# Attention on one Trainium2 core: each query tile's scores in one run of 1280 PSUM columns, with one maximum, one exponential and one sum

## The chip, the core and the metric

The kernel runs as one program on one core of a Trainium2 chip. Five engines work side by side, each through its own instructions strictly in order: PE (TensorE, matmuls and transposes), DVE (VectorE), ACT (ScalarE), POOL (GpSimd) and SP (it issues DMAs). They meet through semaphores. PE writes its results into PSUM, 16 KB for each of 128 partitions, in eight banks of 512 fp32 columns; DVE and ACT read them there. The metric is the device time of one execution in microseconds (us), lower is better.

## The reference, cut to what matters

One layer of a diffusion backbone: a SwiGLU half step, a mixer with 12 heads of latent attention beside a state-space branch, a second SwiGLU half step. All of it is fp32. The change touches only this part, for 1024 query rows (1024 latent tokens) and 1280 keys (256 context tokens and the 1024 latent ones):

```python
def attend(q_nope, q_rope, k_nope, k_rope, v):
    s = (jnp.einsum('bqhd,bkhd->bhqk', q_nope, k_nope)
         + jnp.einsum('bqhr,bkr->bhqk', q_rope, k_rope)).astype(jnp.float32) * ATTN_SCALE
    p = jax.nn.softmax(s, axis=-1).astype(v.dtype)
    return jnp.einsum('bhqk,bkhd->bqhd', p, v)
```

## The kernel before, in words

To keep fp32 accuracy, an operand is split in a high part H and a low part L, and a product is three matmuls (`mm3`: HH, HL, LH, lines 574 to 576). The attention stage runs over 96 query tiles n = 0 to 95 (12 heads with 8 tiles of 128 rows each). For a tile, PE makes 128 x 1280 scores in three chunks: a (512 columns), b (512) and c (256). DVE takes the row maximum, ACT the exponential with that maximum as bias, and the row sum beside it (an ACTIVATE and then an ACTIVATION_READ_ACCUMULATOR); POOL inverts the sum and scales the row. That is the softmax of a tile.

Six tiles later PE begins to turn the probabilities of four tiles (a group) around, one block of 128 keys at a time. I call this step t: four transposes into one of two banks named pt (line 1335), then ACT copies the bank to ptH (line 1338), then DVE subtracts to get ptL (line 59, a helper), which frees the bank. Step v is the two matmuls with the values, o<-ptH and o<-ptL (lines 1349 and 1350). A group has ten steps t and ten steps v, and they alternate. The o bank is copied out by ACT at the end of a group (lines 1357 and 1358).

Nothing is scheduled by a tool here. The order in which each engine gets its instructions is written out in the strings of PLAN, one string for each tile, four strings in a cycle (line 37): a, b and c are chunks of scores of tile n, s is the next step t or v, m and M are the maxima over 1024 and over 256 columns, 1 and 0 are the exponentials over 256 and over 1024 columns of tile n-1, and p is a step of the projections that prepare the next head (queries q, keys k or values v_proj; their results go through the two pt banks too, under the name proj). The tile n=0 uses string 1, n=1 string 2, and so on, so tiles with even n use strings 1 and 3.

PSUM holds the scores in three tiles of the tile framework: scA0 and scA1, 1024 columns each, for even and odd n, and scB, one bank of 512 columns of which even n uses the first 256 and odd n the last 256. The framework adds the semaphore waits: an instruction that writes a tile waits for the readers of what stood there, and so on.

Of the kernel before, what the change touches and what calls it, by code (L numbers as in the profile page):

```python
# [7 lines left out]
F32 = mybir.dt.float32  # L8
F32R = mybir.dt.float32r
I32 = mybir.dt.int32  # L10
AF = mybir.ActivationFunctionType
ALU = mybir.AluOpType
AX = mybir.AxisListType
PSUM = bass.MemoryType.PSUM
DRAM = bass.MemoryType.DRAM
MUL, ADD, SUB, POW = ALU.mult, ALU.add, ALU.subtract, ALU.pow
# [10 lines left out]
NKEY = NT * 128  # L27
# [6 lines left out]
MAGIC = 12582912.0  # L34
GC = 2
LAG = 3
PLAN = "s10bamsspscMs as1ss0bmpcMss s1s0bamspcsMs a10bsmsspcMss".split()
PVLAG = 2
XNP = (1, 3, 5)
XLAG = 2  # L40
# [4 lines left out]
class Kernel:  # L45
# [26 lines left out]
        if name in self.dbg:  # L72
            self.nc.sync.dma_start(self.dbg[name][i], t)

    # ---------------------------------------------------------------- build
    def build(self):
        with self.tc.manual_schedule(), ExitStack() as st:
            self.cst = self.pool(st, "cst")
            self.dram = st.enter_context(self.tc.tile_pool(name="dram", bufs=1, space=DRAM))
            self.small = self.pool(st, "small", bufs=4)  # L80
            ap = self.pool(st, "acc")
            self.flat = ap.tile([128, NT * D], F32, name="acc")
            self.acc = [self.flat[:, t * D:(t + 1) * D] for t in range(NT)]
            self.setup()
            sbig, srow, sattn = ExitStack(), ExitStack(), ExitStack()
            self.big = self.pool(sbig, "big", side="right").tile([128, 80 * 256], F32R, name="big")
            with ExitStack() as sp:
                self.ps = self.pool(sp, "ps", bufs=4, space=PSUM)
                self.ffn1_mix_in(srow)
                self.attn_pools(sattn)  # L90
                self.s5_main(sattn)
            self.attention(sattn)
            srow.close()
            with ExitStack() as sp:
                self.ps = self.pool(sp, "ps2", bufs=4, space=PSUM)
                self.mix_out_ffn2(sbig)
# [37 lines left out]
        self.late = []  # L134
        self.mod = {}

    # ---------------------------------------------------------------- adaln
    def adaln_first(self, pool):
        nc = self.nc
        wm = {}  # L140
# [101 lines left out]
        while self.late:  # L242
            yield 1.0

    # ---------------------------------------------------------------- S5 parameters
    def s5_pre(self, st):
        nc, a = self.nc, self.a
        V, Q = nc.vector, nc.gpsimd
# [275 lines left out]
        self.tt(TB, s, wc, MUL)  # L524
        self.tt(so, TA, TB, ADD)

    # ---------------------------------------------------------------- norm + transpose
    def rstd(self, ss, n, tag):
        w = ss.shape[-1]
        v = self.small.tile([128, w], F32, tag=tag + "v", name="rv")  # L530
        self.ts(v, ss, 1.0 / n, MUL, EPS, ADD)
        r = self.small.tile([128, w], F32, tag=tag + "r", name="rr")
        self.tt(r, v, self.half[:, 0:1].to_broadcast([128, w]), POW, self.nc.gpsimd)
        return r
# [29 lines left out]
            nc.scalar.activation(out=hf[:, :n], in_=t[:, :n], func=AF.Identity, scale=av, bias=bv)  # L564
        self.tt(hL[:, kt, :], hf[:, :n], hH[:, kt, :].bitcast(F32), SUB, nc.gpsimd if kt % 2 else None)

    # ---------------------------------------------------------------- FFN
    def split(self, raw, H, L, eng=None):
        self.nc.scalar.activation(out=H, in_=raw, func=AF.Copy)  # L569
        self.tt(L, raw, H.bitcast(F32), SUB, eng)  # L570
# [331 lines left out]
    def hf(self, pool):  # L902
        return lambda: pool.tile([128, 512], F32, tag="hf", name="hf")

    # ---------------------------------------------------------------- mixer: input projection, latents
    def u_at(self, g):
        return self.acc[(8, 9, 0, 1)[g // 4]][:, 512 + (g % 4) * 128:640 + (g % 4) * 128]

# [114 lines left out]
            for hl in range(2):  # L1023
                self.copy_p(self.kT[1][par][hl][rows], self.kT[0][par][hl][rows].bitcast(F32))

    # ---------------------------------------------------------------- attention: projections
    def attn_pools(self, st):
        nc, a = self.nc, self.a
        wp = self.pool(st, "aw", bufs=2)
# [69 lines left out]
            else:  # L1099
                n -= 1  # L1100

    # ---------------------------------------------------------------- S5
    def s5_main(self, sattn):
        nc, a = self.nc, self.a
        self.proj_bank = lambda: self.bank("gu", "proj")
# [166 lines left out]
            self.prep_steps(1)  # L1272
        self.prep_steps(1000)

    # ---------------------------------------------------------------- attention
    def attention(self, sattn):
        nc, a, acc = self.nc, self.a, self.acc
        Q, V = self.Q, self.V
        self.sq, os, ot = acc[0], acc[8], acc[9]
        P = self.row + [self.flat[:, D + i * NKEY:D + (i + 1) * NKEY] for i in range(4)]  # L1280
        nc.gpsimd.memset(self.sq, 0.0)
        with sattn, ExitStack() as s1:
            psc = self.pool(s1, "psc", space=PSUM)
# [1 line left out]
            ppv = self.pool(s1, "ppv", space=PSUM)  # L1285
            tp = self.pool(s1, "aT", bufs=3)
            P.append(self.pool(s1, "p8").tile([128, NKEY], F32, name="p8"))
            scA = [psc.tile([128, 1024], F32, name=f"scA{i}") for i in range(2)]
            scB = psc.tile([128, 512], F32, name="scB")
            self.proj_bank = lambda: ptp.tile([128, 512], F32, tag="tp", name="proj")  # L1290

            def part(n):
                return scB[:, (n % 2) * 256:(n % 2) * 256 + 256]

            def scores(n, k0, w):
                h, i = divmod(n, 8)
                qs = slice(i * 128, (i + 1) * 128)
                qH, qL = Q[h]
                kH, kL = self.kT[(h // 2) % 2][h % 2]
                o = scA[n % 2][:, k0:k0 + w] if k0 < 1024 else part(n)  # L1300
                ks = slice(k0, k0 + w)
                self.mm3(o, qH[:, qs], qL[:, qs], kH[:, ks], kL[:, ks], True, True)

            Pt, MX = {}, {}

            def rowmax(n, i):
                if i == 0:
                    MX[n] = self.small.tile([128, 2], F32, tag="mx", name="mx")
                nc.vector.tensor_reduce(out=MX[n][:, i:i + 1], in_=part(n) if i else scA[n % 2], axis=AX.X, op=ALU.max,
                                        negate=True)  # L1310
                if i:
                    self.tt(MX[n][:, 0:1], MX[n][:, 0:1], MX[n][:, 1:2], ALU.min)

            SM = {}

            def expo(n, i):
                p, b = P[n % 9], MX[n][:, 0:1]
                if i:
                    SM[n] = self.small.tile([128, 2], F32, tag="sm", name="sm")
                    nc.scalar.activation(out=p[:, 1024:1280], in_=part(n), func=AF.Exp, bias=b, accum_out=SM[n][:, 1:2])  # L1320
                    return
                sm = SM.pop(n)
                nc.scalar.activation(out=p[:, 0:1024], in_=scA[n % 2], func=AF.Exp, bias=b, accum_out=sm[:, 0:1])
                r = self.small.tile([128, 1], F32, tag="mr", name="smr")
                self.tt(sm[:, 0:1], sm[:, 0:1], sm[:, 1:2], ADD, nc.gpsimd)
                self.tt(r, sm[:, 0:1], self.neg1, POW, nc.gpsimd)
                self.ts(p, p, r, MUL, 1.0, MUL, nc.gpsimd)
                Pt[n] = p

# [67 lines left out]
            weights(1)  # L1397
            plan = PLAN
            for n in range(NU + TLAG):
                h, i = divmod(n, 8)  # L1400
                if n < NU and i == 0 and h + 1 < HEADS:
                    for x in prep[h + 1]:
                        next(x)
                    todo = slots(h + 1)
                if n < NU and i == 5:
                    weights(h + 2)
                if n >= TLAG and (n - TLAG) % 4 == 0 and (n - TLAG) // 4 < NU // 4:
                    gr = (n - TLAG) // 4
                    for kt in range(NT):
                        queue.append(("t", gr, kt))  # L1410
                        pend.append(("v", gr, kt))
                        if len(pend) > PVLAG:
                            queue.append(pend.pop(0))
                    if gr == NU // 4 - 1:
                        queue.extend(pend)
                if n < NU:
                    for c in plan[n % len(plan)]:
                        if c == "a":
                            scores(n, 0, 512)
                        elif c == "b":  # L1420
                            scores(n, 512, 512)
                        elif c == "c":
                            scores(n, 1024, 256)
                        elif c == "s":
                            step(1)
                        elif c in "01" and n:
                            expo(n - 1, int(c))
                        elif c == "m":
                            rowmax(n, 0)
                        elif c == "M":  # L1430
                            rowmax(n, 1)
                        elif c == "p" and todo:
                            next(todo.pop(0))
                else:
                    if n == NU:
                        expo(n - 1, 1)
                        expo(n - 1, 0)
                    step(5)
                if n >= 81:
                    next(early, None)  # L1440
# [1 line left out]
                pass  # L1442
            step(1000)

    # ---------------------------------------------------------------- mixer: output, second FFN
    W_AT = ((16, 20), (24, 28), (0, 4), (44, 76), (36, 40), (48, 52), (56, 60), (64, 68))
    O_AT = (32, 34, 8, 14, 10, 12, 72, 74)

# [297 lines left out]
```

## Time and profile before

| What | Before |
|---|---|
| median time of three runs | 2608.74 us (2608.11 to 2609.61) |
| span of the profiled execution | 2608.1 us |
| time of the execution outside the span, by the median | 0.6 us |
| PE busy | 2457.2 us, 94% of the span |
| DVE, POOL, ACT busy | 1711.2, 1091.0, 811.3 us |
| first scores of tile 0 start | 1279.68 us |
| last chunk c of tile 95 ends | 1740.7 us |
| mean granted TensorE clock over the span | 0.981 of full |

The profile shows one execution. Busy times of different engines overlap, so they don't add up to the span; what an engine's wait costs is only seen where the engine that sets the pace sits idle.

### The profile page before, as it was taken

To read this page: it belongs to the slowest core of one execution; us is meant where nothing else is said; L and a number is where in the kernel's file an instruction comes from. 1 tells how busy PE (TensorE), PEld (TensorE's weight loads), DVE (VectorE), ACT (ScalarE), POOL (GpSimd) and SP (SyncE) were. 2 spreads that over 40 slices of the span, in tenths; PEclk is the share of its full clock that TensorE was granted. 3 is DMA by queue.
4 is the path that set the end of the run, shared out by engine and by line. 5 is a ranking of instruction groups with operands and counts; after the bars stand their busy time and mean duration, and the time that the engine had idled before them with its cause. 6 is when DMAs were issued, how large, how long until landed. Compare 5 with 4: busy or idle time off the path is not lost. (4 is left out here: it accounts for less than half of the span.)

```text
span 2608.1 us, 32824 instructions
## 1 busy us (share of the span) xinstructions
PE 2457.2 (94%) x12100; PEld 2009.7 (77%) x12100; DVE 1711.2 (66%) x3096; ACT 811.3 (31%) x1555; POOL 1091.0 (42%) x1010
## 2 busy tenths in 40 slices
PE   7999999998998898898899999989999999999998
PEld 4787888786777677697677777767788888888886
DVE  3588674999999987646688888882444444444433
ACT  4311111111111111343577777772411111111112
POOL 2342222253445345625566676665522222222222
PEclk9999999998999899999999999999999999999999
DMA  7143432112222223414200000014111111111111
GB/s 284 41 153 109 150 110 79 36 46 74 65 74 82 65 66 113 145 26 161 79 6 16 11 16 21 15 61 152 57 57 49 45 45 49 49 49 49 49 41 65
DMA packets 92896, 186.38 MB, mean 71 GB/s; under 512 B 23352, under 2 KB 53304, under 8 KB 91712
## 3 DMA queue, kind: packets, MB, share of 16 engines
q1 hardware_dynamic: 59984, 163.92, 18.3%
q10 hardware_dynamic: 32752, 20.36, 2.5%
q8 instruction: 95, 1.56, 0.2%
q14 instruction: 65, 0.53, 0.1%
HBM read 155.52 MB, written 27.54 MB: 70 GB/s over the span
## 5 line engine op out<-in xcount | busy, mean ns | idle before, releaser
L59 DVE TENSOR_TENSOR acc<-dn,acc 128x512 f32<-128x512 f32 x756 | 509.8, 690 | 282.4 <-PE dn L576 281.9
L59 POOL TENSOR_TENSOR wL<-raw,wH 128x1024 fp32r<-128x1024 f32 x130 | 326.2, 2510 | 762.9 <-ACT wH L569 695.3
L574 PE MATMUL gu<-big,wH 128*128 128x512 f32 (+1 forms) x1056 | 382.8, 363 | 9.0 <-DVE sg L59 6.5
L575 PE MATMUL gu<-big,wH 128*128 128x512 f32 (+1 forms) x1056 | 377.1, 357 | 1.7 <-POOL big L59 1.7
L576 PE MATMUL gu<-big,wL 128*128 128x512 f32 (+1 forms) x1056 | 377.1, 357 | 0.7 <-POOL wL L59 0.7
L574 PE MATMUL dn<-wH,aH 128*128 128x512 f32 x792 | 318.5, 402 | 55.9 <-DVE acc L59 54.9
L575 PE MATMUL dn<-wL,aH 128*128 128x512 f32 x792 | 314.5, 397 | 0.0
L576 PE MATMUL dn<-wH,aL 128*128 128x512 f32 x792 | 314.4, 397 | 0.1
L569 ACT ACTIVATE wH<-raw 128x1024 fp32r<-128x1024 f32 x130 | 137.0, 1054 | 519.5 <-PE dn L576 257.6
L575 PE MATMUL gu<-hL,wH 128*128 128x512 f32 x704 | 276.8, 393 | 3.7 <-POOL hL L59 2.8
L574 PE MATMUL gu<-hH,wH 128*128 128x512 f32 x704 | 277.9, 395 | 0.6 <-ACT hH L559 0.6
L576 PE MATMUL gu<-hH,wL 128*128 128x512 f32 x704 | 276.8, 393 | 0.0
L59 POOL TENSOR_TENSOR aL<-sg,aH 128x512 fp32r<-128x512 f32 (+1 forms) x110 | 137.9, 1263 | 285.5 <-ACT aH L569 285.4
L59 DVE TENSOR_TENSOR sg<-gu,sg 128x512 f32<-128x512 f32 (+1 forms) x110 | 68.1, 634 | 281.4 <-PE gu L576 264.7
L574 PEld LDWEIGHTS gu<-big,wH 128*128 128x128 f32 x1056 | 198.7, 188 | 46.4 <-DVE sg L59 7.0
L575 PEld LDWEIGHTS gu<-big,wH 128*128 128x128 f32 x1056 | 198.7, 188 | 35.8 <-POOL big L59 2.1
L574 PEld LDWEIGHTS dn<-wH,aH 128*128 128x128 f32 x792 | 153.0, 193 | 93.4 <-DVE acc L59 60.7
L576 PEld LDWEIGHTS gu<-big,wL 128*128 128x128 f32 x1056 | 198.5, 188 | 33.5 <-POOL wL L59 1.1
L59 DVE TENSOR_TENSOR ptL<-pt,ptH 128x512 fp32r<-128x512 f32 x240 | 162.9, 686 | 52.9 <-ACT ptH L1338 52.2
L569 ACT ACTIVATE aH<-sg 128x512 fp32r<-128x512 f32 (+1 forms) x110 | 62.9, 587 | 412.9 <-DVE sg L59 399.2
L576 PEld LDWEIGHTS dn<-wH,aL 128*128 128x128 f32 x792 | 152.3, 192 | 34.1 <-POOL aL L59 0.5
L575 PEld LDWEIGHTS dn<-wL,aH 128*128 128x128 f32 x792 | 153.1, 193 | 31.1
(318 smaller groups left out, 4803.1 us busy)
## 6 DMA issues: line engine op xcount, KB each, us to landing
raw<-in_w_gu SPq DMA_DIRECT2D x86, 512.0 KB, 3.2
wmr<-in_w_mod SPq DMA_DIRECT2D x56, 512.0 KB, 4.1
raw<-in_w_down SPq DMA_DIRECT2D x44, 512.0 KB, 3.3
row<-d_s SPq DMA_DIRECT2D x16, 576.0 KB, 3.9
wm<-in_w_mod SPq DMA_DIRECT2D x8, 1024.0 KB, 7.1
d_s<-T ACTq DMA_DIRECT2D x32, 160.0 KB, 2.1
ck<-d_s SPq DMA_DIRECT2D x16, 320.0 KB, 4.9
acc<-in_x SPq DMA_DIRECT2D x8, 512.0 KB, 10.6
```

What stands on the lines that cost most here:

```text
L59: (eng or self.nc.vector).tensor_tensor(out=out, in0=a, in1=b, op=op)
L569: self.nc.scalar.activation(out=H, in_=raw, func=AF.Copy)
L574: mm(out, lhsT=AH, rhs=BH, start=start, stop=False)
L575: mm(out, lhsT=AH, rhs=BL, start=False, stop=False)
L576: mm(out, lhsT=AL, rhs=BH, start=False, stop=stop)
```

## The change

The three PSUM tiles become one, sc, of 2560 columns (five banks). Even tiles use columns 0 to 1279, odd ones 1280 to 2559, so the third bank is shared: its first half belongs to even tiles, its second half to odd ones. The keys of odd tiles are cut at other places so that no chunk crosses a bank: c, the chunk of 256 columns that lies in the shared bank, is still the last one of the tile. One reduction over 1280 columns takes the place of two reductions and a minimum of the two results; one exponential over 1280 columns with its sum takes the place of two; POOL's addition of the two sums is gone. In the strings of PLAN, M is now the only maximum (it stands after c, where the second one stood) and E the only exponential.

```diff
-PLAN = "s10bamsspscMs as1ss0bmpcMss s1s0bamspcsMs a10bsmsspcMss".split()
+PLAN = "sEbasspscMs asEsbspcMss sEsbaspcsMs asEsbsspcMss".split()
+CHUNKS = ({"a": (0, 512), "b": (512, 512), "c": (1024, 256)}, {"a": (256, 512), "b": (768, 512), "c": (0, 256)})
...
-            scA = [psc.tile([128, 1024], F32, name=f"scA{i}") for i in range(2)]
-            scB = psc.tile([128, 512], F32, name="scB")
+            sc = psc.tile([128, 2 * NKEY], F32, name="sc")
...
-            def part(n):
-                return scB[:, (n % 2) * 256:(n % 2) * 256 + 256]
+            def region(n):
+                return sc[:, (n % 2) * NKEY:(n % 2 + 1) * NKEY]
...
-                o = scA[n % 2][:, k0:k0 + w] if k0 < 1024 else part(n)
                 ks = slice(k0, k0 + w)
-                self.mm3(o, qH[:, qs], qL[:, qs], kH[:, ks], kL[:, ks], True, True)
+                self.mm3(region(n)[:, ks], qH[:, qs], qL[:, qs], kH[:, ks], kL[:, ks], True, True)
...
-            def rowmax(n, i):
-                if i == 0:
-                    MX[n] = self.small.tile([128, 2], F32, tag="mx", name="mx")
-                nc.vector.tensor_reduce(out=MX[n][:, i:i + 1], in_=part(n) if i else scA[n % 2], axis=AX.X, op=ALU.max,
-                                        negate=True)
-                if i:
-                    self.tt(MX[n][:, 0:1], MX[n][:, 0:1], MX[n][:, 1:2], ALU.min)
...
+            def rowmax(n):
+                MX[n] = self.small.tile([128, 1], F32, tag="mx", name="mx")
+                nc.vector.tensor_reduce(out=MX[n], in_=region(n), axis=AX.X, op=ALU.max, negate=True)
+
+            def expo(n):
+                p = P[n % 9]
+                sm = self.small.tile([128, 1], F32, tag="sm", name="sm")
+                nc.scalar.activation(out=p, in_=region(n), func=AF.Exp, bias=MX.pop(n), accum_out=sm)
                 r = self.small.tile([128, 1], F32, tag="mr", name="smr")
-                self.tt(sm[:, 0:1], sm[:, 0:1], sm[:, 1:2], ADD, nc.gpsimd)
-                self.tt(r, sm[:, 0:1], self.neg1, POW, nc.gpsimd)
+                self.tt(r, sm, self.neg1, POW, nc.gpsimd)
```

How the instructions and their waits stand in the two built programs is shown at two places. A semaphore is named after the engine that raises it, and the lines of the changed kernel are off by one in the helpers (L574 is L575 there) and by twelve in the steps t and v.

The first place is PE in the kernel before, from the last step t ahead of an odd tile with string 4: the step t, then a and b of the tile (scA_11285 is scA1), then v and t.

```order
L1335 MATMUL pt<-ident,acc 128x128 [waits DVE_49]
L1335 MATMUL pt<-ident,acc 128x128 x3
L574 MATMUL scA_11285<-big,qH 128x512 [waits Activation_49]
L575 MATMUL scA_11285<-big,qH 128x512
L576 MATMUL scA_11285<-big,qL 128x512
L574 MATMUL scA_11285<-big,qH 128x512
L575 MATMUL scA_11285<-big,qH 128x512
L576 MATMUL scA_11285<-big,qL 128x512
L1349 MATMUL o<-ptH,v_11018 128x512 [waits PE_49,Activation_49]
L1350 MATMUL o<-ptL,v_11018 128x512
L1335 MATMUL pt<-ident,acc 128x128 [waits DVE_49]
```

Here a waits for ACT alone; by the value waited for, this is the exponential over 1024 columns of tile n-2, the last reader of scA1. The same place of the changed kernel, on PE:

```order
L1323 MATMUL pt<-ident,acc 128x128 [waits DVE_49]
L1323 MATMUL pt<-ident,acc 128x128 x3
L575 MATMUL sc<-big,qH 128x512 [waits DVE_49]
L576 MATMUL sc<-big,qH 128x512
L577 MATMUL sc<-big,qL 128x512
L1337 MATMUL o<-ptH,v_11018 128x512 [waits PE_49,Activation_49]
L1338 MATMUL o<-ptL,v_11018 128x512
L575 MATMUL sc<-big,qH 128x512 [waits Activation_49]
L576 MATMUL sc<-big,qH 128x512
L577 MATMUL sc<-big,qL 128x512
L1323 MATMUL pt<-ident,acc 128x128 x4
```

The chunk a now waits for DVE, and the step v stands between a and b. By the values waited for, a waits for the maximum of tile n-1 (the reduction over the even half of sc), and b for the exponential of tile n-1. Of the 96 tiles, all 48 odd ones have this wait of a on DVE, and 95 (all but the first) have a wait of their first chunk after E on ACT for the exponential of tile n-1.

The second place is ACT in the kernel before, over the softmaxes of three tiles in a row (acc, p_11283 and then row_9372 are where the probabilities go):

```order
L1320 ACTIVATE acc,sm<-scB,mx 128x256 [waits DVE_49,Pool_49]
L1338 CAST ptH<-pt 128x512 [waits PE_49,Activation_49]
L1323 ACTIVATE acc,sm<-scA_11284,mx 128x1024
L1338 CAST ptH<-pt 128x512 [waits PE_49,Activation_49]
L1338 CAST ptH<-pt 128x512 [waits DVE_49,PE_49]
L1320 ACTIVATE p_11283,sm<-scB,mx 128x256 [waits DVE_49,Pool_49]
L1323 ACTIVATE p_11283,sm<-scA_11285,mx 128x1024
L1338 CAST ptH<-pt 128x512 [waits PE_49,Activation_49]
L1357 COPY acc<-o 64x512 [waits PE_49,Pool_49]
L1358 COPY acc<-o 64x512
```

The exponentials wait for DVE (the maximum) and POOL. The same tiles on ACT in the changed kernel:

```order
L1312 ACTIVATE acc,sm<-sc,mx 128x1280 [waits DVE_49,PE_49,Pool_49]
L1326 CAST ptH<-pt 128x512 [waits PE_49,Activation_49] x2
L1326 CAST ptH<-pt 128x512 [waits DVE_49,PE_49]
L1312 ACTIVATE p_11283,sm<-sc,mx 128x1280 [waits DVE_49,Pool_49]
L1326 CAST ptH<-pt 128x512 [waits PE_49,Activation_49]
L1345 COPY acc<-o 64x512 [waits PE_49,Pool_49]
L1346 COPY acc<-o 64x512
L1326 CAST ptH<-pt 128x512 [waits DVE_49,PE_49]
L1312 ACTIVATE row_9372,sm<-sc,mx 128x1280 [waits DVE_49,PE_49,Pool_49]
```

Every second exponential, that of an even tile n-1, has a wait for PE that was not there: by its value, for the last matmul of chunk a of the odd tile n, which the program issues ahead of it. The copies to ptH that stood between or behind two shorter exponentials now stand behind one longer one.

## Rows read from the trace of the kernel before

**Rows 1.** Busy time by engine from the first scores to the last, with clock:

```profile
core 0: us, PE busy (x) PEld busy (x) DVE busy (x) ACT busy (x) POOL busy (x), PEclk, DMA share, GB/s
1279.68:1740.80 461.12, 433.29 (x2445) 352.08 (x2444) 387.70 (x610) 350.19 (x753) 310.47 (x380) 1.00 0.06 22
```

**Rows 2.** Waits of PE in that stretch: total us, times, longest:

```profile
PE pt L1335 <- DVE ptL L59: 15.2, 31, 1.6
PE scB L574 <- ACT row L1320: 1.1, 3, 0.5
```

**Rows 3.** Groups of DVE and ACT: count, busy us, mean ns:

```profile
L1309 DVE TENSOR_REDUCE mx<-scA 128x1 f32<-128x1024 f32 x96 | 116.7, 1216 | 9.4 <-PE scA L576 8.6
L1309 DVE TENSOR_REDUCE mx<-scB 128x1 f32<-128x256 f32 x96 | 40.1, 417 | 1.2
L59 DVE TENSOR_TENSOR mx<-mx 128x1 f32<-128x1 f32 x96 | 43.2, 450 | 3.3
L59 DVE TENSOR_TENSOR ptL<-pt,ptH 128x512 fp32r<-128x512 f32 x240 | 162.9, 686 | 52.9 <-ACT ptH L1338 52.2
L1338 ACT CAST ptH<-pt 128x512 fp32r<-128x512 f32 x240 | 138.3, 586 | 47.1 <-PE pt L1335 42.6 <-DVE mx L1309 1.1 <-DVE mx L59 1.0
L59 POOL TENSOR_TENSOR sm<-sm 128x1 f32<-128x1 f32 x96 | 18.5, 192 | 108.7 <-ACT row L1323 48.2 <-ACT acc L1323 46.8 <-ACT p L1323 13.0
```

**Rows 4.** Timeline of ACT, softmax of tile 0: start us, duration us:

```profile
1286.79 0.47 ACT L1320 ACTIVATE row<-scB,mx 128x256 f32<-128x256 f32 x1
1287.16 0.19 ACT L1320 ACTIVATION_READ_ACCUMULATOR row<-scB,mx 128x1 f32 x1
1287.26 1.10 ACT L1323 ACTIVATE row<-scA,mx 128x1024 f32<-128x1024 f32 x1
1288.25 0.20 ACT L1323 ACTIVATION_READ_ACCUMULATOR row<-scA,mx 128x1 f32 x1
```

**Rows 5.** Timeline of PE beside it, with idle time and releaser:

```profile
1287.41 0.39 PE L574 MATMUL scB<-big,qH 128*128 128x256 f32 x1 [0.17 <-ACT row L1320]
...
1288.50 0.50 PE L574 MATMUL scA<-big,qH 128*128 128x512 f32 x1 [0.47 <-ACT row L1323]
1288.84 0.40 PE L575 MATMUL scA<-big,qH 128*128 128x512 f32 x1
```

**Rows 6.** Timeline of PE later, steps t and v, then chunk c:

```profile
1523.68 0.27 PE L1335 MATMUL pt<-ident,p 128*128 128x128 f32 x1
1523.79 0.49 PE L1335 MATMUL pt<-ident,row 128*128 128x128 f32 x3
1524.04 0.48 PE L1349 MATMUL o<-ptH,v 128*128 128x512 f32 x1
...
1524.58 0.28 PE L574 MATMUL scB<-big,qH 128*128 128x256 f32 x1
...
1524.82 0.28 PE L576 MATMUL scB<-big,qL 128*128 128x256 f32 x1
1524.93 0.27 PE L1335 MATMUL pt<-ident,p 128*128 128x128 f32 x1
```

**Rows 7.** Timeline of PE, a chunk of 512 columns and the step v behind it:

```profile
1527.50 0.40 PE L574 MATMUL scA<-big,qH 128*128 128x512 f32 x1
...
1527.97 0.40 PE L576 MATMUL scA<-big,qL 128*128 128x512 f32 x1
1528.21 0.40 PE L1349 MATMUL o<-ptH,v 128*128 128x512 f32 x1
```

**Rows 8.** Groups of the projections in that stretch, PE, DVE and ACT:

```profile
L574 PE MATMUL proj<-big,wqH 128*128 128x512 f32 x44 | 18.6, 423 | 1.4 <-ACT wqH L1043 1.2 <-DVE ptL L59 0.2
...
L59 DVE TENSOR_TENSOR big<-proj,big 64x512 fp32r<-64x512 f32 x20 | 13.7, 686 | 6.5 <-ACT big L1073 6.5
...
L1073 ACT CAST big<-proj 64x512 fp32r<-64x512 f32 x20 | 11.6, 580 | 8.4 <-DVE big L59 8.2
```

**Rows 9.** PE alone in two stretches before attention: length, busy, granted clock:

```profile
1190.00:1200.00 10.00, 7.45 (x40) 0.67 0.46 170
...
1240.00:1260.00 20.00, 15.75 (x102) 0.96 0.53 175
```

**Rows 10.** Timeline of PE in an earlier stage, after an idle gap:

```profile
1091.00 0.80 PE L574 MATMUL dn<-wH,aH 128*128 128x512 f32 x1 [2.04 <-DVE acc L59]
1091.59 0.63 PE L575 MATMUL dn<-wL,aH 128*128 128x512 f32 x1
```

More of the change, by code (lines that the diff above doesn't have):

```diff
@@ L36 @@
 LAG = 3
-PLAN = "s10bamsspscMs as1ss0bmpcMss s1s0bamspcsMs a10bsmsspcMss".split()
+PLAN = "sEbasspscMs asEsbspcMss sEsbaspcsMs asEbsspcMss".split()
+CHUNKS = ({"a": (0, 512), "b": (512, 512), "c": (1024, 256)}, {"a": (256, 512), "b": (768, 512), "c": (0, 256)})
 PVLAG = 2
@@ L1299, in scores @@
                 kH, kL = self.kT[(h // 2) % 2][h % 2]
-                o = scA[n % 2][:, k0:k0 + w] if k0 < 1024 else part(n)
                 ks = slice(k0, k0 + w)
-                self.mm3(o, qH[:, qs], qL[:, qs], kH[:, ks], kL[:, ks], True, True)
+                self.mm3(region(n)[:, ks], qH[:, qs], qL[:, qs], kH[:, ks], kL[:, ks], True, True)
             Pt, MX = {}, {}
-            def rowmax(n, i):
-                if i == 0:
-                    MX[n] = self.small.tile([128, 2], F32, tag="mx", name="mx")
-                nc.vector.tensor_reduce(out=MX[n][:, i:i + 1], in_=part(n) if i else scA[n % 2], axis=AX.X, op=ALU.max,
-                                        negate=True)
-                if i:
-                    self.tt(MX[n][:, 0:1], MX[n][:, 0:1], MX[n][:, 1:2], ALU.min)
[L1314 to L1323, printed above, removed]
+            def rowmax(n):
[5 more added lines that the diff above has]
+                nc.scalar.activation(out=p, in_=region(n), func=AF.Exp, bias=MX.pop(n), accum_out=sm)
                 r = self.small.tile([128, 1], F32, tag="mr", name="smr")
-                self.tt(sm[:, 0:1], sm[:, 0:1], sm[:, 1:2], ADD, nc.gpsimd)
-                self.tt(r, sm[:, 0:1], self.neg1, POW, nc.gpsimd)
+                self.tt(r, sm, self.neg1, POW, nc.gpsimd)
                 self.ts(p, p, r, MUL, 1.0, MUL, nc.gpsimd)
@@ L1417, in attention @@
                     for c in plan[n % len(plan)]:
[L1418 to L1423, printed above, removed]
+                        if c in "abc":
+                            scores(n, *CHUNKS[n % 2][c])
                         elif c == "s":
                             step(1)
[L1426 to L1429, printed above, removed]
+                        elif c == "E" and n:
+                            expo(n - 1)
                         elif c == "M":
-                            rowmax(n, 1)
+                            rowmax(n)
                         elif c == "p" and todo:
@@ L1435, in attention @@
                     if n == NU:
-                        expo(n - 1, 1)
-                        expo(n - 1, 0)
+                        expo(n - 1)
                     step(5)
```

## The prediction, made before the changed kernel ran

> **What bounds the kernel now.** The change touches the attention stage alone, so I read that stretch by itself, from the first scores at 1279.68 us to the last chunk of scores at 1740.8. PE is busy for 433.3 of its 461.1 us at the full granted clock [rows 1]; DVE (387.7) and ACT (350.2) have room. So PE sets the pace, and 27.8 us, its idle time, is all that shorter work on other engines can give back there. The waits of PE say where some of that goes: 15.2 us for ptL on DVE before a step t, and about 1 us in the row for the exponentials [rows 2]. PE almost never waits for softmax: the scores of tile n wait for an exponential of n-2 in scA that is long done, and only c shares a PSUM tile with n-1.
>
> **What the change removes.** A tile's maxima now cost DVE 1.216 + 0.417 us and the minimum 0.450 [rows 3]. From the two reductions one column costs (1.216 - 0.417)/768 = 1.04 ns, so 1280 columns cost 1.48 us: 0.60 us less per tile, 58 us over 96 tiles. ACT's two exponentials run from 1286.79 to 1288.45, 1.66 us; alone they take 0.56 and 1.19 to the end of the accumulator's reading [rows 4], so one of 1280 columns takes 1.19 + 0.21 = 1.40: 25 us less in all. POOL saves 0.192 us 96 times, 18 us [rows 3]. All of that is taken from engines that don't set the pace. PE's own matmuls stay the same in number and width.
>
> **What it adds: waits.** The order rows decide this case. In the changed program a of every odd tile waits for the maximum of tile n-1, though it writes other banks; the exponential of n-1 then waits for a; and in every tile the first chunk after E waits for the exponential of n-1. The two halves of sc are one tile for the waits, so the double buffer is gone: scores of n and softmax of n-1 take turns. PE runs in order, so everything behind the waiting chunk, the steps t and v too, is held.
>
> The price of one turn, from rows. A follower starts 0.05 us after its releaser: ACT's reading ends at 1287.35 and 1288.45 [rows 4], PE starts at 1287.41 and 1288.50 [rows 5]. The first matmul after a stall takes 0.34 to the second (1288.50 to 1288.84) [rows 5], others 0.235 (two from 1527.50 to 1527.97), the last one ends 0.40 after its start [rows 7]. From the end of c of n-1 to the first chunk after E:
>
> - even tile n: 0.05 + maximum 1.48 + 0.05 + exponential 1.40 + 0.05 = 3.03 us;
> - odd tile n: 0.05 + 1.48 + 0.05 + a (0.34 + 0.235 + 0.40 = 0.97) + 0.05 + 1.40 + 0.05 = 4.05 us.
>
> PE has little to do meanwhile. A step t takes 0.36 to 0.38 us and a v behind it 0.54 (1523.68, 1524.04, 1524.58) [rows 6], a v behind other matmuls 0.47. Between c and the held chunk stand two to four such steps in an even tile, 1.3 to 1.8 us, and two or three with a in an odd one, some 2.0.
>
> Queues make it longer, so I replay one cycle of four tiles by hand, without projections. Inputs besides those above: c 0.35, its last matmul ending 0.52 after its start [rows 6]; ptH 0.59, ptL 0.69 [rows 3]. Zero is the start of b in the tile with string 1.
>
> - String 1: b and a to 1.51, v to 1.98, t to 2.36 (last transpose ends 2.58), v, c from 2.90 to 3.42. DVE must first do ptL of that t: ptH 2.63 to 3.22, ptL 3.27 to 3.96. Maximum 3.96 to 5.44.
> - String 2: a 5.49 to 6.46, exponential 6.51 to 7.91, b 7.96, v, c ends 9.76, maximum 9.81 to 11.29. PE goes on with t, v, t.
> - String 3: ptH of that last t stands ahead of E and ends at 11.75; exponential to 13.15, b 13.20, a, t, c ends 15.7; ptL of t ends 16.69; maximum to 18.17.
> - String 4: a 18.22, exponential 19.24 to 20.64, b 20.69, t, v, c ends 22.94; ptL to 23.48; maximum to 24.96; exponential 25.01 to 26.41, the next b at 26.46.
>
> So 26.5 us for four tiles, of which PE idles about 10.4 (1.9, 1.2, 1.8, 1.9, 1.3 and 2.4 before the six held chunks). Now it is 461.1/24 = 19.2 with projections.
>
> The sum for the stage:
> - six tiles without t and v: a pair takes 2.03 (b, a, c) + 4.05 + 1.33 (b, c) + 3.03 = 10.4; three pairs 31;
> - 90 tiles: 22.5 x 26.46 = 595;
> - projections stand between b and c, in the path. The q matmuls are 44 x 3 x 0.235 = 31 us [rows 8], those of k and v by their number some 15: 46. Behind a k step four operations follow each other on ACT and DVE (0.58, 0.69, 0.58, 0.69) [rows 8] ahead of the maximum: 2.6 us, where c and ptL already delay it by 0.5 to 1.5. Ten such steps (20 subtractions, two each) at about 1.3, five half as wide and the small delays of q and v: 19 more. Together 65.
>
> That is 691 us for 461, +230. The end of the stage and all before and after it stay. Against the profiled execution (span 2608.1, 0.6 outside it) this gives 2608.7 + 230 = 2839 us; the span and the 0.6 together are the median of the runs, so nothing is to be corrected.
>
> **The clock in the gaps.** PE would now be busy for some 60% of the stage, with gaps of 1.2 to 2.4 us. The trace has such places: 10 us with PE busy 75% were granted 0.67, 20 us with 79% 0.96 [rows 9]; after a gap of 2.04 us two matmuls of 512 columns stand 0.59 apart where 0.235 is usual [rows 10], the level of 1.2 GHz. At that level the scores (7.0 us in four tiles, all in the path) and the v in the path (1.9) double, 1.6 of it hides behind ptL, and projections add 1.9: 9.2 us in four tiles, 221 us if the whole stage ran so. Granted 0.96 means 8% of the time there, 0.67 means 66%. I take 22% (a mean clock of 0.89), nearer to the first, since runs of matmuls stand between the gaps: +49. **Forecast: 2839 + 49 = 2888 us.** The Trainium skill, TensorE: Matmul & The Clock Gate, section "HAM oscillation — how this bites in real kernels", tells of a kernel that idles briefly between groups of matmuls and so swings between both clock levels; the trace agrees in rows 9 and 10.
>
> **The rivals.**
>
> 1. *Only the chains count.* If no queue lengthens a turn, four tiles take 2 x 3.03 + 2 x 4.05 + (3.42 + 1.80 + 2.41 + 2.25, from the held b to the end of c) = 24.0: 31 + 22.5 x 24.0 + 46 = 617, +156, and with a full clock 2765 us. For it: the DVE queue is shorter than before. Against it: ptL stands ahead of the maximum in three strings of four. With the queues and a full clock it is 2839.
> 2. *The clock stays low.* Up to 2839 + 221 = 3060 us. For it: step t is transposes, and the stretch at 0.67 [rows 9] was granted so little at 75% busy. Against it: at the low level PE's share of the time rises again.
> 3. *No slower: the waits find their work done, or only the shared bank matters.* c of tile 1 waited for the exponential of tile 0 at 1287.41 [rows 5], in one shared bank; if that were all, c comes at least 4 us of PE work after the c before it, more than the 3.03 of an even turn, and nothing stalls. Then DVE's 58 us relieve the 15.2 us of waits for ptL [rows 2]: about 2594 us, at best 2608.7 - 27.8 = 2581. It decides where PE has more to do behind c than the turn lasts; there it has 1.3 to 2.0 us for 3.03 to 4.05, so maximum and exponential together would have to take under 1.3 us. Against it above all: the waits on a and b stand in the program. The Trainium skill, PSUM — Partial Sum Buffer, section "PSUM bank collisions raise a hardware error", asks for guarding by bank and quadrant of partitions, not by more; by that rule alone only c would be held, which is this rival. What the changed program waits for is wider than the rule, and no run here shows the rule itself.
>
> **How the numbers follow.** Forecast (turns, queues, a clock that falls now and then, 2850 to 2985): 0.60. Rival 1, from 2765 to 2850: 0.22. Rival 2, 2985 to 3060: 0.10. Rival 3: 0.05, split between faster and the same. The rest, 0.03, is above or between. The range 2790 to 2985 leaves out the low end of rival 1 (0.05), rival 2 and rival 3. A change under 0.2% (5 us) can't be told from none here; 0.95 or a little more stands on the slower side beyond that, 0.03 on the faster.
>
> **What would show it.** PE's waits: sc for DVE mx 48 times, near 1.9 us each, some 90 us; sc for ACT's exponential 95 times, 1.2 to 2.4 each, some 160 us. PE busy hardly changed, unless the clock falls; the stage near 690 us at full clock and 740 with the fall. Reductions of 1.48 us, DVE 58 us less busy. Wrong would be: PE waiting for sc a few us in all (rival 3); idle time under 170 us in the stage (rival 1); a granted clock under 0.75 in it (rival 2).

## The result and the profile after

The changed kernel takes 2895.6 us (median of four runs, 2893.7 to 2897.2) where the kernel before takes 2609.2 beside it: 1.110 times as long, 95% interval 1.108 to 1.111. The forecast was 2888 us, within 2790 to 2985. The profiled execution took 2893.7 us, with a span of 2891.9. (In the diff ahead of the prediction the fourth string of the new PLAN has one s too many; it reads `asEbsspcMss`, and that is the order that the prediction replayed.)

The attention stage by itself, from the first scores to the last, in the profile of the changed kernel, and three stretches of 50 us, two in it and one behind it. The first two columns are the stretch and its length; PEclk is the granted clock.

```profile
core 0: us, PE busy (x) PEld busy (x) DVE busy (x) ACT busy (x) POOL busy (x), PEclk, DMA share, GB/s
1278.10:2025.90 747.80, 524.74 (x2444) 403.98 (x2443) 339.36 (x421) 334.73 (x565) 295.22 (x289) 0.89 0.04 13
1280.00:1330.00 50.00, 28.91 (x94) 21.51 (x95) 14.92 (x16) 15.78 (x25) 16.30 (x20) 0.76 0.02 7
1480.00:1530.00 50.00, 33.77 (x152) 25.64 (x151) 22.94 (x30) 23.15 (x40) 18.28 (x19) 0.86 0.02 5
2030.00:2080.00 50.00, 45.38 (x228) 35.39 (x229) 18.69 (x33) 17.79 (x34) 18.82 (x19) 1.00 0.50 171
```

The same 2444 PE instructions that filled 433 of 461 us [rows 1] now stand in 748 us. So the stage is 286.7 us longer, and the whole span 283.8 (2891.9 against 2608.1): all of the loss lies here. PE sits idle for 223 us of the stage, and it is busy 91 us longer with the same work; the clock in the stage is 0.89, and the run with filled gaps below shows that this is the reason. Behind the stage it is 1.00 again. (In every run on record the time is 1.8 to 2.1 us above its span. The 0.6 us in the table of the kernel before are the distance of the median from the span of one execution, and no time outside it. The forecast starts from the median and does not change by this.)

What PE waits for from 1279 to 2030 us: total us, times, longest.

```profile
PE sc L575 <- DVE mx L1307: 77.6, 48, 2.9
PE sc L575 <- ACT row L1312: 64.7, 42, 3.3
PE sc L575 <- ACT acc L1312: 57.7, 40, 2.6
PE sc L575 <- ACT p L1312: 13.2, 10, 2.5
...
PE pt L1323 <- DVE ptL L60: 1.4, 4, 0.6
```

Chunks of scores wait 48 times for the maximum and 92 times for an exponential (row, acc and p are where the probabilities go), 213 us together; the kernel before had about 1 us in such a row [rows 2], and 3.2 us in its three rows of this kind. The wait for ptL has gone from 15.2 us to 1.4: DVE now has time, and it is of no use.

The operations themselves, by groups (count, busy us, mean ns, then the idle time before them), answer to rows 3 and 4:

```profile
L1307 DVE TENSOR_REDUCE mx<-sc 128x1 f32<-128x1280 f32 x96 | 142.6, 1486 | 27.5 <-PE sc L577 26.0
L575 PE MATMUL sc<-big,qH 128*128 128x512 f32 (+1 forms) x288 | 132.2, 459 | 213.2 <-DVE mx L1307 77.6 <-ACT row L1312 64.7 <-ACT acc L1312 57.7
L1312 ACT ACTIVATE row<-sc,mx 128x1280 f32<-128x1280 f32 x44 | 58.5, 1330 | 40.4 <-PE sc L577 34.3 <-DVE mx L1307 5.6 <-issue 0.2
```

The change does what it says: one maximum of 1.49 us for 1.22 + 0.42 + 0.45, 57 us less work for DVE (200.0 us in three groups [rows 3], 142.6 now). DVE's busy time in the stage falls by less, from 387.7 to 339.4 us, since records that overlap count once there.

### The profile page after: what moved, and what is told of

The parts are those of the page before. It is cut to its first block, busy times and chain, and to the rows that moved or that the text cites. A ratio compares the mean times of both kernels' runs of the same rounds, so it can differ in the third digit from the quotient of the medians.

```text
span 2891.9 us, 32498 instructions
## 1 busy us (share of the span) xinstructions
PE 2544.4 (88%) x12100; PEld 2059.2 (71%) x12100; DVE 1662.6 (57%) x2904; ACT 795.0 (27%) x1363; POOL 1071.2 (37%) x914
## 5 line engine op out<-in xcount | busy, mean ns | idle before, releaser
L575 PE MATMUL gu<-big,wH 128*128 128x512 f32 (+1 forms) x1056 | 383.6, 363 | 9.1 <-DVE sg L60 6.5
L575 PE MATMUL dn<-wH,aH 128*128 128x512 f32 x792 | 318.2, 402 | 56.1 <-DVE acc L60 55.0
L575 PE MATMUL sc<-big,qH 128*128 128x512 f32 (+1 forms) x288 | 132.2, 459 | 213.2 <-DVE mx L1307 77.6
L575 PE MATMUL gu<-hH,wH 128*128 128x512 f32 x704 | 277.5, 394 | 0.0
L575 PEld LDWEIGHTS sc<-big,qH 128*128 128x128 f32 x288 | 60.8, 211 | 265.0 <-DVE mx L1307 89.0
L60 POOL TENSOR_TENSOR aL<-sg,aH 128x512 fp32r<-128x512 f32 (+1 forms) x110 | 137.9, 1263 | 286.7 <-ACT aH L570 286.6
L575 PEld LDWEIGHTS gu<-big,wH 128*128 128x128 f32 x1056 | 199.4, 189 | 46.5 <-DVE sg L60 7.0
L575 PEld LDWEIGHTS dn<-wH,aH 128*128 128x128 f32 x792 | 152.6, 193 | 93.4 <-DVE acc L60 60.7
L1326 ACT CAST ptH<-pt 128x512 fp32r<-128x512 f32 x240 | 139.4, 584 | 250.3 <-PE pt L1323 249.6
```

The costliest lines, as they stand in the source:

```text
L60: (eng or self.nc.vector).tensor_tensor(out=out, in0=a, in1=b, op=op)
L575: mm(out, lhsT=AH, rhs=BH, start=start, stop=False)
L1326: nc.scalar.copy(H, p)
```

## The experiments

**One tile, nothing merged.** The kernel before, only with its three PSUM tiles as parts of one:

```diff
-            scA = [psc.tile([128, 1024], F32, name=f"scA{i}") for i in range(2)]
-            scB = psc.tile([128, 512], F32, name="scB")
+            sc = psc.tile([128, 2 * NKEY], F32, name="sc")
+            scA = [sc[:, 0:1024], sc[:, 1536:2560]]
+            scB = sc[:, 1024:1536]
```

> The kernel before with its own strings, two maxima and two exponentials per query tile; only the three PSUM tiles scA0, scB and scA1 become parts of one tile of five banks. Theory 1 (the waits of one tile cost the 286 us; merging the operations costs nothing): slow like the changed kernel, 2850 to 3000 us, PE waiting for sc some 150 to 250 us. Theory 2 (the long single operations hold up the queues of DVE and ACT, and the tile does not matter): 2609 us, within 0.3%.

Measured: 2949.7 us, 1.130 times the kernel before (1.127 to 1.132). The waits of PE in its stage:

```profile
PE sc L574 <- ACT row L1324: 86.7, 44, 3.6
PE sc L574 <- ACT acc L1324: 79.9, 41, 2.8
PE sc L574 <- DVE mx L1310: 49.3, 57, 1.9
```

With ACT's third row (18.0 us, for p) that is 234 us. Three lines that merge nothing and leave the order of the instructions as it was cost more than the whole change: PE idles 243 us in this stage, at a granted clock of 0.87 (223 and 0.89 in the changed kernel). So the loss does not need the longer operations; it comes from the tile by which waits are made.

**The waits between the halves taken away.** The changed kernel, in which chunks a and b of tile n, and the maximum and exponential of n-1, which lie in different banks, no longer wait for each other. Only c, in the shared bank, waits for the exponential of n-1:

```diff
+                if w == 512:
+                    AB.setdefault(n, []).extend(mms)
+                    for m in mms:
+                        for r in RD.get(n - 1, ()):
+                            self.free(m, r)
...
+                for m in AB.get(n + 1, ()):
+                    self.free(e, m)
...
+    def free(self, later, earlier):
+        self.tc.declare_no_dep(later.ins, earlier.ins, reason="other columns, other banks")
```

> The changed kernel with everything merged and one PSUM tile, but the waits between chunks a and b of tile n and the maximum and exponential of tile n-1, which lie in other columns and other banks, are declared needless; only c, in the shared bank, still waits for the exponential of n-1. Theory 1 (the waits alone cost the time): 2585 to 2612 us, likeliest 2594 (the 15 us of waits for ptL eased by 58 us less on DVE), PE's waits for sc under 10 us, granted clock 1.00 in the stage. Theory 2 (the long operations cost too): 2620 to 2680 us, with PE waiting for pt and ptH more than the 15 us of before.

Measured: 2630.3 us, 1.008 times the kernel before (1.0065 to 1.0092). It gives back 265 of the 286 us, so the waits are most of the loss. But it is 20 us slower than the kernel before beside it (2610.1), with DVE far less busy: outside the range of theory 1 (2585 to 2612) and inside that of theory 2 (2620 to 2680). Its waits and, in its first tiles, the chunk c (start us, duration us, then idle time and releaser):

```profile
PE sc L575 <- ACT row L1321: 10.0, 10, 1.7
PE o L1349 <- ACT acc L1358: 9.5, 17, 1.1
PE proj L575 <- DVE ptL L60: 6.6, 10, 1.0
PE sc L575 <- ACT acc L1321: 6.0, 8, 1.8
PE pt L1335 <- DVE ptL L60: 5.3, 14, 1.0
```
```profile
1288.53 0.39 PE L575 MATMUL sc<-big,qH 128*128 128x256 f32 x1 [1.02 <-ACT row L1321]
1292.26 0.38 PE L575 MATMUL sc<-big,qH 128*128 128x256 f32 x1 [1.70 <-ACT row L1321]
1295.98 0.39 PE L575 MATMUL sc<-big,qH 128*128 128x256 f32 x1 [1.70 <-ACT row L1321]
```

Theory 1 holds for most of the time but not for the rest. Theory 2 has the time, but not by its mechanism (PE waits less for pt, not more). So 20 us stay to be explained. Three places show: c waits 16.8 us for the exponential (2.1 before), nearly half of it in the first six tiles (7.9 us), where PE has no steps t and v to do and the turn from c to c is 3.72 us; the copies of o on ACT come late (9.5 us, 2.8 before); the projections wait for ptL (6.6 us, 0.2 before).

**Chunk a behind the exponential.** The changed kernel with other strings for the odd tiles:

```diff
-PLAN = "sEbasspscMs asEsbspcMss sEsbaspcsMs asEbsspcMss".split()
+PLAN = "sEbasspscMs sEsabspcMss sEsbaspcsMs sEabsspcMss".split()
```

> The changed kernel with chunk a of the odd tiles moved behind the exponential E, so that the exponential of n-1 no longer waits for a, and a, b and c all wait for the exponential as in even tiles. Theory 1 (chains: an odd turn falls from 4.05 to 3.03 us, but a then stands behind it, 0.7 us): 2876 to 2890 us, likeliest 2882, that is 0.3 us times 48 less than the changed kernel; the waits for the maximum on DVE go to nearly nothing and those on ACT rise by some 60 us. Theory 2 (the wait for the maximum is what costs, and without it the time goes): 2820 us or less, 78 us less waiting.

Measured: 2896.9 us, 1.110 (1.109 to 1.112), the same as the change itself. Theory 2 is out: the wait for the maximum is gone, and the time is not. Theory 1 is right about where the waits go, and wrong about the time, which did not fall. The stage became 745.9 us long (747.8), 1.9 shorter where 13 were expected.

```profile
PE sc L575 <- ACT row L1312: 90.7, 44, 3.8
PE sc L575 <- ACT acc L1312: 80.6, 41, 3.2
PE o L1337 <- ACT acc L1346: 25.6, 23, 1.9
```

With the row for p (18.6) scores wait 190 us for ACT instead of 136. Worked out from the starts of c in both traces, tiles 8 to 95, the turn that ends with string 2 became 0.26 us shorter on the mean (7.01 to 6.75), as the chain says, and the one that ends with string 4 became 0.23 longer (8.80 to 9.03). In string 4 the chunk a had stood behind the end of a group; now the first step v of the next group comes there and waits for ACT to copy o, 22 times in the stage (the 23rd wait of the row lies behind it). Whether that wait alone makes the turn longer stays open.

**The gaps filled.** The changed kernel, with extra matmuls in PE's idle time ahead of held chunks. They write where the chunk itself, which starts anew, writes next; they do not wait:

```diff
+                if n and w == 512 and (n % 2 or k0 == 512):
+                    for _ in range((5 if n % 2 == 0 else 5 if k0 == 256 else 2)):
+                        d = self.nc.tensor.matmul(region(n)[:, ks], lhsT=qH[:, qs], rhs=kH[:, ks], start=True, stop=True)
+                        AB.setdefault(n, []).append(d)
+                        for r in RD.get(n - 1, ()):
+                            self.free(d, r)
```

> The changed kernel with idle PE time ahead of the held chunks filled: five extra matmuls of 512 columns ahead of b in even tiles, five ahead of a and two ahead of b in odd ones (1.18 and 0.47 us at full clock), written to where the chunk itself is written right after, and free of the waits; the held chunks wait as before. Theory 1 (some 49 us of the loss are the clock that falls in the gaps): granted clock 0.98 or more in the stage, 2840 to 2860 us. Theory 2 (the fall costs nothing on the path, since PE waits anyway): 2890 to 2905 us whatever the clock. Theory 3 (the extra matmuls only lengthen the path): 2910 us or more.

Measured: 2839.1 us, 1.088 (1.086 to 1.089). With 571 matmuls more than the change, it is 56.5 us faster. Its stage:

```profile
1278.10:1971.50 693.40, 593.49 (x3015) 451.41 (x3014) 338.60 (x421) 334.36 (x565) 293.24 (x289) 1.00 0.04 15
```

The clock in the stage is 1.00, and the stage 54.4 us shorter than in the changed kernel. Of PE's busy time in it 163 us are the extra matmuls; what remains, some 430 us, is as in the kernel before (433), and the 91 us that the changed kernel had on top are gone. The restart after a wait is not what was saved, for PE still waits ahead of 131 held chunks (140 in the changed kernel). Added work does not shorten a path; the clock that it holds up does. The time lies 1 us below the range of theory 1, with its mechanism; theories 2 and 3 are out.

**What merging costs by itself: a control, and each part alone.** For the 20 us that stayed, three kernels in the layout of the change, with PE's waits as they were before or only c held. The control merges nothing:

```diff
+                mms = self.mm3(region(n)[:, ks], qH[:, qs], qL[:, qs], kH[:, ks], kL[:, ks], True, True)
...
+                for m in mms:
+                    for r in RD.get(n - 1, ()) if w == 512 else BIG.get(n - 1, []) + BIG.get(n, []):
+                        self.free(m, r)
```

> Control: one PSUM tile of five banks in the layout of the change, but two maxima and two exponentials per query tile in the order of the kernel before, and the waits between parts in different banks declared needless, so that PE's waits are those of the kernel before. Theory 1 (the first kernel with one tile lost its time by these waits alone): 2609 us within 0.3%. Theory 2 (the layout itself, or the odd tiles' other cut of the keys, costs): 2620 us or more.

Measured: 2649.0 us, 1.0145 (1.013 to 1.016). It is no control yet, since DVE has a wait that the kernel before has not: the maximum of n waits for the exponential of n-1.

```profile
DVE mx L1326 <- ACT row L1343: 33.4, 37, 3.1
DVE mx L1326 <- ACT acc L1343: 22.8, 32, 1.2
```

Part by part, with the merged maximum alone (the strings of before without m) and the merged exponential alone (the strings of the change with m behind a and b), the first tries had the same stray wait, 6.4 us of it on DVE with the merged maximum and 36.4 us with the merged exponential:

> As the control, but with one merged maximum (behind c) and two exponentials, that over the 256 columns of the shared bank first. Theory 1 (what the merged kernel with freed halves lost, 20 us, is the way from c over maximum and exponential to the next c in the shared bank; here it is 1.48 + 0.56 us with the exponential's small part first, against 1.48 + 1.40 there and 0.42 + 0.45 + 0.56 before): c waits some 3 us in all, DVE does 58 us less: 2598 to 2612 us. Theory 2 (the one long maximum holds the queue of DVE and with it ptL): 2620 us or more, PE waiting for pt longer than the 15 us of before.

Measured: 2632.8 us, 1.008 (1.007 to 1.0095).

> As the control, but with two maxima (the large one ahead of c) and one merged exponential. Theory 1 (the way from c to the next c is here 0.42 + 0.45 + 1.40 us, between the other two): c waits some 5 us in all, and the copies of o behind the longer exponential some 5 to 10 us: 2612 to 2625 us. Theory 2 (the merged exponential costs nothing, the merged maximum is the cause): 2609 us within 0.3%.

Measured: 2632.3 us, 1.008 (1.007 to 1.009). Neither says what merging costs while that wait is in it. So the three again without it (the cut shown is that of the two kernels with two maxima; the third frees its one maximum in the same way):

```diff
+                for e in RD.get(n - 1, ()):
+                    if e not in MAXI:
+                        self.free(r, e)
+                MAXI.append(r)
```

> The control again: the first one turned out to have a wait that the kernel before has not (the maximum of tile n on DVE for the exponential of tile n-1 on ACT, 62 us of it in its trace). It is declared needless too (both only read, other columns); now DVE, PE and ACT wait as in the kernel before. Theory 1 (one tile costs only through its waits): 2609 us within 0.3%. Theory 2 (the layout itself costs): still 2640 us or more.

Measured: 2608.6 us (11 runs), 1.000 (0.9991 to 1.0009): theory 1. One tile, five banks, the odd tiles' other cut of the keys cost nothing; its waits are all. Between the two controls stands a single kind of wait, and it is worth some 38 us (1.0145 and 1.000 times the kernel before beside each). In the two kernels below the same wait turns out to have cost next to nothing (1.0081 with it and 1.0073 without, 1.0082 and 1.0075): how long a wait is on its own engine does not say what it costs. The stage of the good control, and its wait for ptL, are those of before:

```profile
1279.80:1740.20 460.40, 433.41 (x2444) 351.98 (x2443) 387.55 (x610) 350.23 (x753) 310.59 (x380) 1.00 0.07 22
```
```profile
PE pt L1362 <- DVE ptL L60: 16.6, 33, 1.2
```

> Two maxima and one merged exponential, without that wait of the maximum for the exponential of tile n-1 (36 us on DVE in the first try). Theory 1 (the merged exponential costs by itself, through c in the shared bank, 9 us, and the copies of o behind it, 7 us): 2615 to 2627 us. Theory 2 (the first try was slow by the stray wait alone): 2609 us within 0.3%.

Measured: 2628.8 us, 1.007 (1.006 to 1.009), 2 us above the range of theory 1, with its two waits:

```profile
PE o L1367 <- ACT acc L1376: 8.5, 16, 1.1
PE sc L575 <- ACT row L1341: 7.5, 7, 1.6
PE pt L1353 <- DVE big L60: 7.5, 7, 1.4
PE proj L575 <- DVE ptL L60: 6.1, 9, 0.9
PE pt L1353 <- DVE ptL L60: 4.3, 9, 0.9
PE sc L575 <- ACT acc L1341: 4.2, 6, 1.6
```

> One merged maximum and two exponentials, without the stray wait (6 us on DVE in the first try, mostly in the first tiles). Theory 1 (the merged maximum costs by itself: all its 1.48 us lie behind c, in front of ptL, where 0.42 + 0.45 stood before): 2620 to 2633 us, with PE waiting some 20 us for pt and 10 us for the projections. Theory 2 (stray wait): 2609 us within 0.3%, or faster, since DVE has 58 us less to do.

Measured: 2629.7 us, 1.0075 (1.006 to 1.009), theory 1, and its stage:

```profile
PE pt L1354 <- DVE ptL L60: 19.0, 32, 0.9
PE proj L575 <- DVE ptL L60: 8.8, 10, 1.3
```
```profile
1282.00:1760.00 478.00, 437.13 (x2445) 351.69 (x2444) 339.50 (x420) 352.14 (x753) 309.47 (x380) 1.00 0.06 21
```

These three views of waits run from 1278 to 1765 us, and 25 us of that lie behind the control's stage. The following figures are taken within each stage.

For the merged maximum, DVE is 48 us less busy than in the control (339.5 against 387.6), and yet PE waits longer for DVE: 26.2 us for ptL (17.4 ahead of steps t, 8.8 ahead of projections) against 14.3. The work is less, but all 1.48 us of it stand in one piece between c and the next ptL. These waits are 11.8 us of the 17.6 by which the stage is longer than the control's, and PE's busy time is 3.7.

For the merged exponential (stage 478.2 us, 17.8 longer), scores wait 11.7 us, all of it at c (3.3 in the control, 2.1 of it at c), PE waits 8.5 us for the copies of o (1.9), and behind the k step (big) 7.5 us (5.0). That is 17.5 us more, of which ptL gives 5.7 back (8.6 for 14.3), and PE's busy time is 5.2 longer (438.6).

The parts do not add up: each costs 20 us, and both together, in the second experiment, 20. Why not more stays open, and so does why PE's busy time grows with the same work at full clock. No version here is faster than the kernel before.

## Why the prediction was right, point by point

- **The cause** is shown: the two halves of sc are one tile for the waits, so scores of n and softmax of n-1 take turns. The first experiment makes the loss without the merge; the second takes 265 of the 286 us away with the merge and the tile left as they are; the control without the stray wait takes all of it away with one tile and no merge.
- **The replay of four tiles** held turn by turn. The last cycle of the changed kernel, with no projections and the clock full until its end (the held chunks; in brackets idle time and releaser):

```profile
2001.86 0.50 PE L575 MATMUL sc<-big,qH 128*128 128x512 f32 x1 [2.00 <-ACT row L1312]
2004.73 0.28 PE L575 MATMUL sc<-big,qH 128*128 128x256 f32 x1
...
2005.74 1.48 DVE L1307 TENSOR_REDUCE mx<-sc 128x1 f32<-128x1280 f32 x1
...
2007.28 0.50 PE L575 MATMUL sc<-big,qH 128*128 128x512 f32 x1 [1.60 <-DVE mx L1307]
...
2008.33 1.33 ACT L1312 ACTIVATE row<-sc,mx 128x1280 f32<-128x1280 f32 x1 [0.98 <-PE sc L577]
2009.56 0.19 ACT L1312 ACTIVATION_READ_ACCUMULATOR row<-sc,mx 128x1 f32 x1
...
2009.80 0.50 PE L575 MATMUL sc<-big,qH 128*128 128x512 f32 x1 [0.65 <-ACT row L1312]
...
2014.91 0.50 PE L575 MATMUL sc<-big,qH 128*128 128x512 f32 x1 [1.53 <-ACT row L1312]
...
2019.86 0.50 PE L575 MATMUL sc<-big,qH 128*128 128x512 f32 x1 [1.60 <-DVE mx L1307]
...
2022.39 0.79 PE L575 MATMUL sc<-big,qH 128*128 128x512 f32 x1 [1.10 <-ACT acc L1312]
2022.98 0.63 PE L576 MATMUL sc<-big,qH 128*128 128x512 f32 x1
```

| held chunk, us after b of string 1 | a, string 2 | b, string 2 | b, string 3 | a, string 4 | b, string 4 |
|---|---|---|---|---|---|
| replayed | 5.49 | 7.96 | 13.20 | 18.22 | 20.69 |
| measured (less 2001.86) | 5.42 | 7.94 | 13.05 | 18.00 | 20.53 |

This is one cycle. In the run with filled gaps, with the clock full, the last three cycles have no projections; from the c of tile 83 to those of 87, 91 and 95 they take 26.33, 26.29 and 26.29 us, and 26.46 were forecast.

- **The durations**: maximum 1.48 us forecast, 1.486 measured; exponential with its reading 1.40, here 2008.33 to 2009.75, 1.42.
- **The stage at full clock**: 691 us forecast, 693.4 with the gaps filled. With it rival 1 (617 us, no queues) is out.
- **The clock**: 0.89 forecast and 0.89 granted; +49 us forecast, 54.4 in the stage. That the clock falls in such gaps was read from rows. How far it falls was a choice between 0.96 and 0.67 [rows 9], and that it came out to the second digit is luck. The first matmuls of the last chunk show the step: 2022.39 stands 0.59 us ahead of the next, where 0.34 is the distance at 2.4 GHz, so this is the level of 1.2 GHz, after waits of 0.65 to 2.00 us in every turn. Rival 2 (under 0.75) is out. The Trainium skill, TensorE: Matmul & The Clock Gate, section "A second HAM failure mode: psum-queue depth-cycling", tells of a kernel that goes round the banks of PSUM and whose PE idles briefly and often between groups of matmuls, so that the clock swings and throughput falls. The run with filled gaps agrees, with 56.5 us as the price here. This is nearer to the present case than the section named in the prediction, whose kernel waits for DMAs between its groups.
- **The waits** were a little too large as sums: 90 us and 160 us forecast, 77.6 and 135.6 measured, 1.6 us for the maximum instead of 1.9. I counted idle time from where the next matmul would usually start, the trace counts from the modelled end of the last one, some 0.15 us later. That makes 7 of the 12 us and 14 of the 24; it moves the split between busy and idle, not the turn. The rest stays open.
- **DVE** was to be 58 us less busy. Its operations are 57 us less as groups, its busy time in the stage 48 (387.7 and 339.4).
- **Rival 3**, that only the shared bank matters and nothing stalls, was priced at 2594 us. Where only c is held the time is 2630. The step that fails in it is that c comes at least 4 us of PE work after the c before: in the first six tiles PE has no t and v, in the kernel before c follows c there after 2.60 us (1287.41 [rows 5] to 1290.01), and 3.72 us with the merged operations is the turn itself. The waits of c later on, 8.9 us, were not followed to a cause. The other step, that less work on DVE eases ptL, fails for the maximum alone (26.2 us for 14.3). The Trainium skill, PSUM — Partial Sum Buffer, section "PSUM bank collisions raise a hardware error", asks for guards by bank and quadrant of partitions; the control keeps the waits within a bank, drops those between banks, and stands at the time of before: what costs here is the part of the waits that is wider than a bank. No run tried a guard narrower than a bank.

## What to carry to other kernels

Before buffers are put into one tile so that an operation can span them, look at which instructions then wait for which: the tile is what a wait is made for, and here a double buffer was lost without a line that says so. Work taken from engines that do not set the pace was worth nothing here. One long operation in place of two short ones can cost, since it lies whole on the way from the last input to the next release: each merge alone cost 20 us, and PE's idle time in the stage grew by 13 and 14 us. Where waits open gaps on PE, count the fallen clock as a term of its own (here 54 of 287 us).

## What the hardware showed that I had not expected

Extra matmuls made the changed kernel faster: 571 of them, 163 us of PE's busy time, brought the clock in the stage from 0.89 to 1.00 and the time from 2895.6 to 2839.1 us. And two merges that take 57 us from DVE, or a second exponential per tile from ACT, each made the kernel 0.7% slower with the double buffer intact, and no slower together than one of them alone.
